# The second score matmul of the first layer's heads, run over all 128 rows

## The chip, the cores and the metric

The kernel runs on one core of a Trainium2 chip. The metric is the time of one execution in device microseconds (us). In the profile, PE is the matmul engine (TensorE) and PEld its weight loads, DVE is VectorE, ACT is ScalarE, POOL is GpSimd, and SP is the engine that issues most of the loads. The first operand of a matmul is held in the array (the weight load puts it there), the second streams past it; an array shape such as `64*128` in the profile says how many rows and columns of the array the instruction uses.

## The reference, cut to what matters

The program is an encoder of two layers over 256 tokens of 1024 values, all in float32. What the change touches is the attention of layer 0: sixteen heads of 64 values each, eight of mixer A (grouped queries, two key heads) and eight of mixer B (windowed, with a bias by distance).

```python
def gqa_attention(q, k, v):                     # mixer A
    ...
        logits = jnp.einsum('bqgrd,bkgd->bgrqk', qb, k).astype(jnp.float32) * scale
        p = jax.nn.softmax(logits, axis=-1).astype(v.dtype)
        return jnp.einsum('bgrqk,bkgd->bqgrd', p, v)

def dilated_attention(q, k, v, rel_bias):       # mixer B, for each of three branches
    ...
            logits = jnp.einsum('bqhd,bqkhd->bhqk', qb, kg).astype(jnp.float32) * scale
            logits = jnp.where(valid[None, None], logits + bias[None, :, None, :], NEG_INF)

# layer 0
proj = hn @ ab_w_in[j]
qa, ka, va, qb, kb, vb = jnp.split(proj, split_ab, axis=-1)
...
mix = jnp.concatenate([o_a, o_b], axis=-1) @ ab_w_out[j]
h = h + mix
h = h + jnp.square(jax.nn.relu(hn @ mlp_w1[layer])) @ mlp_w2[layer]
```

Layer 1 has a latent attention with sixteen heads and an MLP of the same form.

## The kernel before, in words

A value is kept as the sum of two parts, a high part in the short float type that the array takes at full pace (`fp32r`) and a low part, the rest. A product of two such sums is three matmuls into one bank (`mm3`, L263 to L265): high by high, high by low, low by high. The weights stream in as chunks of 1 MB on SP's queue, and ACT (L222) and DVE (L223) split each into its two parts, some quarters of a chunk ahead of use.

For the scores of a head (64 values) two matmuls do for three. `stack` (L708) puts the high part of a query head into its own half of the 128 rows (rows 0 to 63 for side s = 0, 64 to 127 for s = 1) and its low part into the other half. The high part of the keys stands in both halves (`kdA`, `kdB`). So the first score matmul (L847), over all 128 rows, gives (high + low of the query) by the high part of the key. The second (L848) uses only the 64 rows of the head's own half, `q[s][own, ...]`, and streams the low part of the keys in the same rows (`klA`, `klB`). Both are done for two blocks of 128 queries, so a head has four of them, in turn, into one bank `s`; 256 keys are 256 columns.

The low parts are written by one DVE operation over all 128 rows for mixer A (L775) and one for each pair of heads' half of mixer B (L820), each right behind an ACT copy of the high part over all 128 rows (L774, L819). In these tiles the rows of side 0 belong to even heads and those of side 1 to odd ones.

The heads run as a pipeline (`attention`, L340). In the turn of head h, PE transposes its normalised probabilities (L391), then scores head h + 2 (there are two `s` banks), and every second turn adds the weighted values of a pair of heads (L380), which use the array as `128*64`. DVE takes maxima (L418; L864 with the bias for mixer B) and normalises (L364); ACT takes the exponentials (L423, L873) and copies the transposes (L394). Between these, PE is given parts of a "filler" by head: the projections of mixer B's second half and its values, then the first half of the output projection (matmuls of 512 columns).

The order on each engine is laid out by a planner before the program runs: it goes by the order of the program text, raised or lowered by `high_priority` around some calls, and by its own costs of the instructions; the loops at the start are under `manual_schedule` and keep the written order. Engines run their queues in order.

The lines that the change touches: the tiles of layer 0 (L629, L633, L635, L641), the rotating buffer `work` (L195), `mixer_a_keys` (L771 to L778), the end of `qk_b` (L815 to L823), `scores_two` (L841) and its two callers (L853, L876). POOL fills the rotary tables `tab` from the loaded gains `gaq` and the constants `kc` (L725 to L730).

Of the kernel before, what the change touches and what calls it, by code (L numbers as in the profile page):

```python
# [20 lines left out]
P = 128  # L21
# [24 lines left out]
def shape_constants():  # L46
    """Rotary tables, the relative-position buckets and the branch counts: of the shapes alone."""
    f = np.float32
# [44 lines left out]
def weight_chunks():  # L93
    """The order in which the weights stream in: (name, columns used)."""
    order = [("qA", 0), ("qA", 1), ("kvA", 0)]
    order += [("qkB", i) for i in range(4)] + [("vB", 0), ("vB", 1)]
    order += [("outA", i) for i in range(4)]
    for l in range(2):
        if l == 1:
            order += [("down", 0), ("down", 1), ("uq", 0), ("uq", 1), ("ukv", 0)]  # L100
            order += [("outC", i) for i in range(4)]
        for u in range(17):
            if u < 16:
                order.append((f"w1_{l}", u))
            if u > 0:
                order.append((f"w2_{l}", u - 1))
    return order
# [11 lines left out]
def pack_weights(ab_w_in, ab_w_out, c_w_down, c_w_uq, c_w_ukv, c_w_out, mlp_w1, mlp_w2):  # L119
    """All weights in the order of their use, each chunk as 128 partition rows."""  # L120
    win, wout = ab_w_in[0], ab_w_out[0]
# [45 lines left out]
def encoder(ctx: ExitStack, tc: tile.TileContext, x, xt, wall, gcol, grow, const, onehot, relb, out):  # L167
# [26 lines left out]
    def work():  # L194
        return sp.tile([P, 512], F32, name="work", tag="work", bufs=6)  # L195

    def halves(z):
        return z.rearrange("p (m t) -> p m t", m=2)

# [1 line left out]
    raws, parts, done = {}, {}, set()  # L201
# [10 lines left out]
    def split_piece():  # L212
        """The next quarter of a chunk as two parts; of a chunk of the MLPs, the next half."""
        i, q = divmod(at["piece"], 4)
        n = 2 if i >= 5 else 1
        at["piece"] += n
        if q % 2 == 0:
            parts[i, q // 2] = [wp.tile([P, CW // 2], F32R, name=z, tag=z, bufs=W_BUFS) for z in ("whi", "wlo")]
        hi, lo = parts[i, q // 2]
        raw = raws[i][:, 512 * q:512 * (q + n)]  # L220
        s = slice(512 * (q % 2), 512 * (q % 2 + n))
        nc.scalar.copy(hi[:, s], raw)  # L222
        nc.vector.tensor_tensor(lo[:, s], raw, hi[:, s].bitcast(F32), op=OP.subtract)  # L223
        if q + n == 4:
            load(i + RAW_BUFS)
# [10 lines left out]
    def quarter(n=2):  # L236
        """A quarter of a chunk has been used."""
        at["quarter"] += 1
        pump(n)

    def take(name, j, n, whole=True):
        """A chunk of n row blocks: its operands by row block and columns."""
        i = at["take"]
        assert ORDER[i] == (name, j), (ORDER[i], name, j)
        at["take"] += 1
        while whole and at["piece"] < 4 * i + 4:
            split_piece()

        def operand(k, c=slice(None)):
            half, kk = divmod(k, n // 2)  # L250
            return tuple(z.rearrange("p (k c) -> p k c", k=n // 2)[:, kk, c] for z in parts[i, half])

        return i, operand
# [6 lines left out]
    def mm3(out, a, b, first, last):  # L260
        """out += a.T @ b, of operands that are each a sum of two parts."""
        (ah, al), (bh, bl) = a, b
        nc.tensor.matmul(out, ah, bh, start=first, stop=False)  # L263
        nc.tensor.matmul(out, ah, bl, start=False, stop=False)  # L264
        return nc.tensor.matmul(out, al, bh, start=False, stop=last)  # L265
# [6 lines left out]

# [1 line left out]
    g = cp.tile([P, N_G], F32, name="g")  # L274
# [32 lines left out]
    def rsqrt(u, n, dst):  # L307
        """u ** -0.5, with one Newton step behind the power."""
        y, z = (small(16)[:, :n] for _ in range(2))
# [11 lines left out]
    def mean_square(name):  # L321
        """mean(h * h) + eps, a column for each token block."""
        part, u = small(4), cp.tile([P, NT], F32, name=f"u{name}")
# [8 lines left out]
    def row_scales(bank, which, columns):  # L332
        """Values by token, spread over all partitions with the tokens along the row."""
        for t in range(NT):
# [3 lines left out]

# [1 line left out]
    def attention(heads, fill, dst):  # L340
# [34 lines left out]
        def values(j):  # L375
            """The weighted values of a pair of heads, side by side in the array."""
            ob = o_bank()
# [34 lines left out]
    def scaled_softmax(scale, nscale):  # L412
        """exp(scale * (s - max)) and its sums, the scale by query."""
        nb = {}
# [21 lines left out]
    def turn(c, t, gbase):  # L436
        """Half a token block of the residual stream, transposed, gained and split."""
        with tc.high_priority():
# [12 lines left out]
    class Later:  # L451
        """The turn of the last group, given out while the next one is computed."""
        todo = None
# [170 lines left out]

# [1 line left out]
    with tc.tile_pool(name="l0", bufs=1) as lp:  # L626
        qA = [lp.tile([P, 4, S], F32R, name=f"qA{s}") for s in range(2)]
        kdA = lp.tile([P, 2, S], F32R, name="kdA")
        klA = lp.tile([P, S], F32R, name="klA")  # L629
        vA = lp.tile([P, NT, P], F32, name="vA")  # L630
        qB = [lp.tile([P, 4, S], F32R, name=f"qB{s}") for s in range(2)]
        kdB = lp.tile([P, HB, S], F32R, name="kdB")
        klB = lp.tile([P, 4, S], F32R, name="klB")  # L633
        vB = lp.tile([P, NT, 512], F32, name="vB")
        tab = lp.tile([P, 4, NT, 64], F32, name="tab")  # L635
        rs_b = lp.tile([P, S], F32, name="rs_b")
# [3 lines left out]
        rq0 = lp.tile([P, NT], F32, name="rq0")  # L640
        gaq = lp.tile([P, P], F32, name="gaq")  # L641
        rb = lp.tile([NUM_BUCKETS + 1, HB], F32, name="rb")
# [5 lines left out]
        nc.vector.memset(rb, 1.0)  # L648
        nc.gpsimd.dma_start(rb[:NUM_BUCKETS, :], relb)

        # q, then k and v, of mixer A
        acc = [mm_bank() for _ in range(NT)]
# [37 lines left out]
        def load_bias(j):  # L690
            """rel_bias by distance, with the branch counts; query rows run backwards."""
            bias[j] = lp.tile([P, 2, 3 * P], F32, name="bias", tag="bias", bufs=2)
            nc.sync.dma_start(bias[j], bass.AP(tensor=line_d.tensor, offset=line_d.offset + 4 * S * j,
                                               ap=[[1, P], [2 * S, 2], [1, 3 * P]]))
# [13 lines left out]
        def stack(dst, src, col):  # L708
            """Rows of two heads, each as its high part beside its low part in the other rows."""
            for s in range(2):  # L710
# [49 lines left out]
        def mixer_a_keys(rk):  # L760
# [10 lines left out]
            for s in range(2):  # L771
                own, other = cols(s, 64), cols(1 - s, 64)
                if s == 0:
                    nc.scalar.copy(kdA[:, s], pk[:, :S])  # L774
                    nc.vector.tensor_tensor(klA, pk[:, :S], kdA[:, s].bitcast(F32), op=OP.subtract)  # L775
                else:
                    nc.scalar.copy(kdA[own, s], pk[own, :S])
                nc.scalar.copy(kdA[other, s], pk[own, :S])  # L778
            yield

        def qk_b(half, bank):
# [33 lines left out]
            for s in range(2):  # L815
                own, other = cols(s, 64), cols(1 - s, 64)
                hs = slice(4 * half + s, 4 * half + s + 3, 2)
                if s == 0:
                    nc.scalar.copy(kdB[:, hs], halves(kf))  # L819
                    nc.vector.tensor_tensor(klB[:, two], halves(kf), kdB[:, hs].bitcast(F32), op=OP.subtract)  # L820
                else:
                    nc.scalar.copy(kdB[own, hs], halves(kf[own]))
                nc.scalar.copy(kdB[other, hs], halves(kf[own]))  # L823
# [17 lines left out]
        def scores_two(q, kd, kl, s, j, order):  # L841
            own = cols(s, 64)

            def f(sb):
                for i in range(NT):
                    o = sb[:, cols(i, S)]
                    nc.tensor.matmul(o, q[s][:, j, cols(order[i])], kd, start=True, stop=False)  # L847
                    nc.tensor.matmul(o, q[s][own, j, cols(order[i])], kl, start=False, stop=True)  # L848
            return f

        def head_a(h):
            j, s = divmod(h, 2)
            return {"scores": scores_two(qA, kdA[:, s], klA[cols(s, 64)], s, j, (0, 1)),  # L853
                    "v": lambda c: vA[:, c, cols(s, 64)],
                    **scaled_softmax(fq[:, 2 * j + s], nfq[:, 2 * j + s])}

        def head_b(h):
# [13 lines left out]
            def ex(n, sb, p, l):  # L871
                for i in range(NT):
                    nc.scalar.activation(p[:, i], p[:, i], AF.Exp, bias=nb[0][:, i:i + 1],  # L873
                                         accum_out=l[:, i:i + 1])

            return {"scores": scores_two(qB, kdB[:, h], klB[cols(s, 64), j], s, j, (1, 0)), "max": mx, "exp": ex,  # L876
                    "v": lambda c: vB[:, c, cols(h, 64)], "flip": True}
# [44 lines left out]

# [1 line left out]
    with tc.tile_pool(name="l1", bufs=1) as lp:  # L924
# [194 lines left out]
```

## Time and profile before

| | before |
|---|---|
| time, median of 3 runs | 593.35 us (592.43 to 595.54) |
| profiled execution: span from its first to its last instruction | 591.9 us |
| profiled execution: its own time | not recorded; the span is 1.45 us under the median |
| PE busy | 578.0 us, 98% of the span |
| DVE, ACT, POOL busy | 364.7 (62%), 324.1 (55%), 35.0 us (6%) |
| mean granted TensorE clock | 0.994 of full speed |
| instructions | 8924 |

The profile is of one execution. Busy time of an engine is the time in which at least one of its instructions runs. Matmuls overlap: one may be listed with 0.28 us and the next start 0.12 us behind its start, so the pace of PE is read from the distances between starts, not from the durations. The heads of layer 0 lie between 53 and 120 us of the span, their scores between 53.1 and 104.1 us.

### The profile page before, as it was taken

How to read it: one execution, taken by the hardware profiler on the slowest of the kernel's cores; microseconds unless marked ns; L12 is line 12 of the kernel's file. 1: busy time of each engine (PE TensorE's matmuls, PEld its weight loads, DVE VectorE, ACT ScalarE, POOL GpSimd, SP SyncE). 2: the span in 40 equal slices, each digit the busy share in tenths (PEclk: the TensorE clock that was granted, in tenths of full speed). 3: DMA queues.
4: the chain of work that ended last, by engine and by line, in shares of the span. 5: the costliest groups of instructions: out<-in, count | busy, mean ns of one | idle time of the engine just before them, and what ended most of it. 6: DMA issues, size and time to landing. Idle time of an engine off the chain costs nothing.

```text
span 591.9 us, 8924 instructions
## 1 busy us (share of the span) xinstructions
PE 578.0 (98%) x3553; PEld 493.9 (83%) x3553; DVE 364.7 (62%) x583; ACT 324.1 (55%) x550; POOL 35.0 (6%) x70
## 2 busy tenths in 40 slices
PE   7989999999999999999999999999999999999994
PEld 3889665689998998898889987779899889989984
DVE  4888776586545546555468888757555645555425
ACT  5768875564444444435447498836444444544414
POOL 1480000000000000000002200000000000000003
PEclk9989999999999999999999999999999999999998
DMA  8955133135454555545544323146454554554201
GB/s 277 406 200 214 71 137 131 73 142 187 170 205 163 201 174 186 210 157 200 195 161 163 123 73 142 35 145 204 159 206 158 198 206 155 209 181 174 73 1 71
DMA packets 16602, 96.69 MB, mean 163 GB/s; under 512 B 1922, under 2 KB 3970, under 8 KB 5808
## 3 DMA queue, kind: packets, MB, share of 16 engines
q1 hardware_dynamic: 15984, 94.92, 43.9%
q0 software_dynamic: 288, 0.68, 0.5%
q8 instruction: 28, 0.46, 0.3%
q10 hardware_dynamic: 288, 0.52, 0.2%
q14 instruction: 14, 0.11, 0.1%
HBM read 95.05 MB, written 1.06 MB: 162 GB/s over the span
## 4 chain that ended last, share of the span: by engine, by line
PE 88%; ACT 3%; DMA 3%; DVE 2%; POOL 2%; issue 1%; SPq 1%; POOLq 0%; DVEq 0%; ACTq 0%
PE mm L263 15%; PE mm L264 15%; PE mm L265 14%; PE s L263 10%; PE s L264 10%; PE s L265 10%; PE o L380 3%; DMA raw<-in_wall 3%; PE o L391 3%; PE s L1075 2%; PE s L848 2%; PE s L847 1%; PE o L441 1%; DVE wlo L223 1%; ACT whi L222 1%
## 5 line engine op out<-in xcount | busy, mean ns | idle before, releaser
L223 DVE TENSOR_TENSOR wlo<-raw,whi 128x1024 fp32r<-128x1024 f32 (+1 forms) x182 | 208.9, 1165 | 150.3 <-ACT whi L222 150.1
L222 ACT CAST whi<-raw 128x1024 fp32r<-128x1024 f32 (+1 forms) x182 | 178.4, 1002 | 155.2 <-issue 66.3
L263 PE MATMUL s<-hT,whi 128*128 128x256 f32 x512 | 145.6, 284 | 0.0
L264 PE MATMUL s<-hT,whi 128*128 128x256 f32 x512 | 145.4, 284 | 0.0
L265 PE MATMUL s<-hT,wlo 128*128 128x256 f32 x512 | 145.2, 284 | 0.0
L264 PE MATMUL mm<-wlo,h2h 128*128 128x512 f32 x252 | 100.5, 399 | 0.0
L263 PE MATMUL mm<-whi,h2h 128*128 128x512 f32 x252 | 99.7, 396 | 0.0
L263 PEld LDWEIGHTS s<-hT,whi 128*128 128x128 f32 x512 | 98.4, 192 | 1.5
L264 PEld LDWEIGHTS s<-hT,whi 128*128 128x128 f32 x512 | 98.4, 192 | 1.3
L265 PEld LDWEIGHTS s<-hT,wlo 128*128 128x128 f32 x512 | 98.4, 192 | 0.1
L265 PE MATMUL mm<-whi,h2l 128*128 128x512 f32 x252 | 98.3, 393 | 0.0
L265 PEld LDWEIGHTS mm<-whi,h2l 128*128 128x128 f32 x252 | 47.3, 188 | 11.5 <-DVE h2l L514 0.4
L263 PEld LDWEIGHTS mm<-whi,h2h 128*128 128x128 f32 x252 | 47.4, 188 | 11.2 <-ACT h2h L513 0.7
L264 PEld LDWEIGHTS mm<-wlo,h2h 128*128 128x128 f32 x252 | 47.3, 188 | 9.5
L513 ACT CAST h2h<-work 128x512 fp32r<-128x512 f32 x32 | 19.9, 621 | 42.0 <-DVE work L510 42.0
L514 DVE TENSOR_TENSOR h2l<-work,h2h 128x512 fp32r<-128x512 f32 x32 | 22.2, 692 | 20.6 <-ACT h2h L513 20.6
L263 PE MATMUL mm<-whi,OT 128*128 128x512 f32 x64 | 26.9, 421 | 0.0
L510 DVE TENSOR_TENSOR work<-work 128x512 f32<-128x512 f32 x32 | 21.9, 685 | 7.7 <-ACT work L509 7.7
L264 PE MATMUL mm<-wlo,OT 128*128 128x512 f32 x64 | 25.8, 406 | 0.0
L265 PE MATMUL mm<-whi,OT 128*128 128x512 f32 x64 | 25.4, 401 | 0.0
L263 PE MATMUL mm<-whi,hT 128*128 128x512 f32 (+1 forms) x64 | 23.0, 360 | 2.3 <-ACT hT L663 2.2
L394 ACT COPY pts<-o 128x512 f32<-128x512 f32 x32 | 18.7, 589 | 10.9 <-PE o L391 10.8
(229 smaller groups left out, 770.6 us busy)
## 6 DMA issues: line engine op xcount, KB each, us to landing
raw<-in_wall SPq DMA_DIRECT2D x84, 1024.0 KB, 4.8
bias<-line_d SPq DMA_DIRECT2D x4, 384.0 KB, 3.5
raw<-in_wall SPq DMA_DIRECT2D x4, 256.0 KB, 5.5
raw<-in_wall SPq DMA_DIRECT2D x2, 512.0 KB, 7.7
xh<-in_x SPq DMA_DIRECT2D x1, 1024.0 KB, 10.7
xT<-in_xt SPq DMA_DIRECT2D x1, 512.0 KB, 6.9
kc<-in_const SPq DMA_DIRECT2D x1, 512.0 KB, 9.8
grw<-in_grow POOLq DMA_DIRECT2D x1, 512.0 KB, 4.8
```

What stands on the lines that cost most here:

```text
L222: nc.scalar.copy(hi[:, s], raw)
L223: nc.vector.tensor_tensor(lo[:, s], raw, hi[:, s].bitcast(F32), op=OP.subtract)
L263: nc.tensor.matmul(out, ah, bh, start=first, stop=False)
L264: nc.tensor.matmul(out, ah, bl, start=False, stop=False)
L265: return nc.tensor.matmul(out, al, bh, start=False, stop=last)
L380: nc.tensor.matmul(ob[64 * s:64 * s + 64, :S], heads[2 * j + s]["v"](c), pts[2 * j + s][:, cols(c, S)], start=c == 0, stop=c == NT - 1)
L391: turned = nc.tensor.transpose(pt[:, c * S + q * P:c * S + q * P + P], prob[h][:, i, cols(c)], flip if flipped else ident)
L394: nc.scalar.copy(pts[h], pt)
L510: nc.vector.tensor_tensor(r, r, r, op=OP.mult)
L513: nc.scalar.copy(hi, halves(r))
L514: nc.vector.tensor_tensor(lo, halves(r), hi.bitcast(F32), op=OP.subtract)
L848: nc.tensor.matmul(o, q[s][own, j, cols(order[i])], kl, start=False, stop=True)
```

## The change

The low parts of the keys get a tile row set for each side or head: `klA` has two entries of 256 columns instead of one, `klB` eight instead of four. In each, only the head's own half of the rows is written by DVE, and the other half is set to zero once, by POOL, at the start. The second score matmul then takes all 128 rows of the queries and of the low parts. The high parts are copied by halves of the rows for both sides, where side 0 used one copy over all rows before. The tables `tab` and `gaq` move into a tile `early` that shares its place with the second output tile `OT1`, and `work` has five buffers instead of six. Comment lines and docstrings are left out of the diff.

```diff
     def work():
-        return sp.tile([P, 512], F32, name="work", tag="work", bufs=6)
+        return sp.tile([P, 512], F32, name="work", tag="work", bufs=5)
...
         kdA = lp.tile([P, 2, S], F32R, name="kdA")
-        klA = lp.tile([P, S], F32R, name="klA")
+        klA = lp.tile([P, 2, S], F32R, name="klA")
...
-        klB = lp.tile([P, 4, S], F32R, name="klB")
+        klB = lp.tile([P, HB, S], F32R, name="klB")
         vB = lp.tile([P, NT, 512], F32, name="vB")
-        tab = lp.tile([P, 4, NT, 64], F32, name="tab")
+        early = ap.tile([P, 5 * P], F32, name="early", tag="OT1")
+        tab = early[:, :4 * P].rearrange("p (a t e) -> p a t e", a=4, t=NT)
+        gaq = early[:, 4 * P:]
...
-        gaq = lp.tile([P, P], F32, name="gaq")
...
         nc.gpsimd.dma_start(rb[:NUM_BUCKETS, :], relb)
+        for s in range(2):
+            other = slice(64 - 64 * s, 128 - 64 * s)
+            nc.gpsimd.memset(klA[other, s].bitcast(F32), 0.0)
+            nc.gpsimd.memset(klB[other, s::2].bitcast(F32), 0.0)
...
             for s in range(2):
                 own, other = cols(s, 64), cols(1 - s, 64)
-                if s == 0:
-                    nc.scalar.copy(kdA[:, s], pk[:, :S])
-                    nc.vector.tensor_tensor(klA, pk[:, :S], kdA[:, s].bitcast(F32), op=OP.subtract)
-                else:
-                    nc.scalar.copy(kdA[own, s], pk[own, :S])
+                nc.scalar.copy(kdA[own, s], pk[own, :S])
+                nc.vector.tensor_tensor(klA[own, s], pk[own, :S], kdA[own, s].bitcast(F32), op=OP.subtract)
                 nc.scalar.copy(kdA[other, s], pk[own, :S])
...
-                if s == 0:
-                    nc.scalar.copy(kdB[:, hs], halves(kf))
-                    nc.vector.tensor_tensor(klB[:, two], halves(kf), kdB[:, hs].bitcast(F32), op=OP.subtract)
-                else:
-                    nc.scalar.copy(kdB[own, hs], halves(kf[own]))
+                nc.scalar.copy(kdB[own, hs], halves(kf[own]))
+                nc.vector.tensor_tensor(klB[own, hs], halves(kf[own]), kdB[own, hs].bitcast(F32), op=OP.subtract)
                 nc.scalar.copy(kdB[other, hs], halves(kf[own]))
...
         def scores_two(q, kd, kl, s, j, order):
-            own = cols(s, 64)
-
             def f(sb):
                 for i in range(NT):
                     o = sb[:, cols(i, S)]
                     nc.tensor.matmul(o, q[s][:, j, cols(order[i])], kd, start=True, stop=False)
-                    nc.tensor.matmul(o, q[s][own, j, cols(order[i])], kl, start=False, stop=True)
+                    nc.tensor.matmul(o, q[s][:, j, cols(order[i])], kl, start=False, stop=True)
             return f
...
-            return {"scores": scores_two(qA, kdA[:, s], klA[cols(s, 64)], s, j, (0, 1)),
+            return {"scores": scores_two(qA, kdA[:, s], klA[:, s], s, j, (0, 1)),
...
-            return {"scores": scores_two(qB, kdB[:, h], klB[cols(s, 64), j], s, j, (1, 0)), "max": mx, "exp": ex,
+            return {"scores": scores_two(qB, kdB[:, h], klB[:, h], s, j, (1, 0)), "max": mx, "exp": ex,
```

## Rows read from the trace of the kernel before

**Rows 1.** The page: busy time by engine, and the chain that ended last.
```profile
PE 578.0 (98%) x3553; PEld 493.9 (83%) x3553; DVE 364.7 (62%) x583; ACT 324.1 (55%) x550; POOL 35.0 (6%) x70
...
PE 88%; ACT 3%; DMA 3%; DVE 2%; POOL 2%; issue 1%; SPq 1%; POOLq 0%; DVEq 0%; ACTq 0%
```

**Rows 2.** Stretches: length, each engine's busy time (instructions), clock, DMA share, GB/s.
```profile
59.66:87.81 28.15, 28.15 (x137) 18.76 (x135) 21.86 (x66) 22.27 (x54) 0.00 (x0) 1.00 0.28 95
53.10:104.10 51.00, 50.92 (x243) 33.50 (x242) 36.21 (x106) 37.41 (x91) 0.00 (x0) 1.00 0.38 139
...
87.81:96.24 8.43, 8.43 (x41) 5.30 (x40) 5.04 (x19) 6.35 (x18) 0.00 (x0) 1.00 0.39 152
96.24:102.85 6.61, 6.61 (x30) 3.47 (x28) 3.58 (x11) 2.83 (x7) 0.00 (x0) 1.00 0.41 159
```

**Rows 3.** PE's timeline: start, duration, line, operands, array shape, moving operand.
```profile
52.59 0.28 PE L265 MATMUL mm<-hT,wlo 128*128 128x256 f32 x1
52.71 0.28 PE L263 MATMUL mm<-hT,whi 128*128 128x256 f32 x1
...
59.66 0.28 PE L847 MATMUL s<-kdA,qA 128*128 128x256 f32 x1
59.88 0.38 PE L848 MATMUL s<-klA,qA 64*128 64x256 f32 x1
60.19 0.39 PE L847 MATMUL s<-kdA,qA 128*128 128x256 f32 x1
60.50 0.38 PE L848 MATMUL s<-klA,qA 64*128 64x256 f32 x1
60.81 0.50 PE L265 MATMUL mm<-whi,hT 128*128 128x512 f32 x1
61.15 0.40 PE L263 MATMUL mm<-whi,hT 128*128 128x512 f32 x1
61.38 0.39 PE L264 MATMUL mm<-wlo,hT 128*128 128x512 f32 x1
```

**Rows 4.** The second score matmul (L848): count, ns min/median/max, first and last start.
```profile
L848 PE MATMUL s<-klA,qA x16: 378/380/382, 53.5 to 77.6; 64*128 64x256 f32 x16
...
L848 PE MATMUL s<-klB,qB x16: 379/380/384, 79.9 to 103.8; 64*128 64x256 f32 x16
```

**Rows 5.** PE's timeline in head 14, weighted values and a low-part matmul.
```profile
99.19 0.65 PE L380 MATMUL o<-pts,vB 128*64 128x256 f32 x2
99.77 0.38 PE L848 MATMUL s<-klB,qB 64*128 64x256 f32 x1
```

**Rows 6.** Groups of 53.1 to 104.1 us, weight loads: busy us, mean ns | idle.
```profile
L264 PEld LDWEIGHTS mm<-hT,whi 128*128 128x128 f32 x6 | 1.1, 191 | 0.0
```

**Rows 7.** Timelines of PE and DVE: head 7's last score matmul and its normalisation.
```profile
77.64 0.38 PE L848 MATMUL s<-klA,qA 64*128 64x256 f32 x1
...
83.00 0.62 DVE L364 TENSOR_SCALAR prob<-prob,sm 128x256 f32<-128x256 f32 x2
```

**Rows 8.** Waits of 53 to 106 us: who <- for whom: us in total, times, longest.
```profile
ACT pts L394 <- PE o L391: 6.6, 10, 1.4
DVE sm L418 <- PE s L848: 4.6, 3, 1.8
```

**Rows 9.** The subtractions that write the low parts: count, ns min/median/max, starts.
```profile
L775 DVE TENSOR_TENSOR klA<-o,kdA x1: 425/425/425, 51.8 to 51.8; 128x256 fp32r<-128x256 f32 x1
...
L820 DVE TENSOR_TENSOR klB<-work,kdB x2: 684/688/691, 45.8 to 62.7; 128x512 fp32r<-128x512 f32 x2
```

**Rows 10.** POOL's timeline: a memset, and the rotary tables behind the idle time.
```profile
0.77 0.20 POOL L303 MEMSET ones<- 128x128 f32 x1
...
18.02 2.14 POOL L728 TENSOR_TENSOR tab<-kc,gaq 128x64 f32<-128x64 f32 x1 [14.87 <-DMA kc<-in_const]
...
20.55 0.31 POOL L728 TENSOR_TENSOR tab<-kc,gaq 128x64 f32<-128x64 f32 x1
```

**Rows 11.** Groups of 53.1 to 104.1 us: the splits' low parts on DVE.
```profile
L223 DVE TENSOR_TENSOR wlo<-raw,whi 128x1024 fp32r<-128x1024 f32 x11 | 13.3, 1219 | 0.0
```

## The prediction

> **What bounds the kernel now.** I began with the page: its first part gives each engine's share of the span, its fourth the chain of work that ended last. TensorE (PE) is busy for 578.0 of 591.9 us, and the chain is 88% PE [rows 1]. So a microsecond of PE work that disappears is worth up to a microsecond of the whole, wherever PE has no gaps. The table of busy time by stretch then shows the stage that the change touches: the sixteen heads of the first layer run from 53.1 to 104.1 us, and PE is busy for 50.92 of these 51.00 us; ACT and DVE are well under that, but not far (37.41 and 36.21) [rows 2].
>
> "Busy" is not "at full pace", so I read PE's timeline in that stretch by the distance from one start to the next. In an ordinary run of 256-column matmuls over 128 rows, starts are 0.12 us apart (52.59 to 52.71), and a 512-column one takes 0.23 (61.15 to 61.38) [rows 3]. Around the scores the pace is another: in head 2 the starts go 59.66, 59.88, 60.19, 60.50, 60.81, 61.15, so that four 256-column matmuls and the 512-column one behind them take 1.49 us instead of 4 x 0.12 + 0.23 = 0.71 [rows 3]. The slow steps are those at which the array changes between `128*128` and `64*128`, in either direction. The excess, 0.78 us over four changes, is 0.195 us a change.
>
> **The change part by part.**
>
> *The second score matmul over 128 rows.* There are 16 + 16 of these, all `64*128` today [rows 4], so 64 changes of shape at most. Going through the PE timeline head by head, 59 of them have a `128*128` neighbour on the other side and go away. Five have the weighted values there, which run as `128*64`: four around the two low-part matmuls of head 14 (99.77 stands right behind 99.19 [rows 5]) and one behind head 9, of the same kind; these stay changes of some kind, and I count nothing for them. 59 x 0.195 = 11.5 us of PE time. The bounds for the new matmul: a step of 0.12 us, as in the plain run, or 0.31 as today (59.88 to 60.19) [rows 3], which makes the gain 11.5 or 0. I take 0.12, because type, columns and rows are then the same as in the plain run. Twice as many rows is not twice as much work: the steps of that run are 0.12 with 128 rows in use.
>
> A weight load is one possible reason for the 0.31 that would not go away. The trace shows loads of 191 ns in the plain runs too, at steps of 0.12 [rows 3, 6]; they lie beside the matmul ahead.
>
> The Trainium skill ("TensorE: Matmul & The Clock Gate", Part 3, The mechanism) says that weight loads overlap running matmuls only when their row groups differ. By that rule a low-part matmul over all rows would show its load, and there would be nothing to gain; the trace does not agree, since rows of 128 everywhere go at 0.12.
>
> *How much of the 11.5 us is kept.* PE is the last to end only as long as ACT and DVE keep up, so I split the stage. Heads 0 and 1: 8 changes, 1.6 us; heads 2 to 10 (59.66 to 87.81): 35 changes, 6.8 us; heads 11 to 15: 16 changes, 3.1 us. In the middle part PE would need 28.15 - 6.8 = 21.3 us, while ACT needs 22.27 and DVE 21.86 [rows 2] plus 0.69 for one more subtraction (below), 22.55. So at most 28.15 - 22.55 = 5.6 us are kept there. The lower end comes from the handing round between engines: head 7's scores end at 78.02 (77.64 + 0.38) and its probabilities are normalised at 83.62, 5.6 us later [rows 7]; PE turns them two heads behind the scores. If that lag stayed, a head could not take less than 2.8 us, against 28.15 / 9 = 3.13 now: 9 x 0.33 = 3.0 us kept. I take 5.0, near the upper end, because much of ACT's and DVE's idle time is spent waiting for PE itself (6.6 us for the transposes, 4.6 for the last score matmul) [rows 8]; the lag shrinks when PE does. Behind 87.81, ACT has 6.35 of 8.43 us and then 2.83 of 6.61, DVE 5.04 and 3.58 [rows 2]; 3.1 us fit. Sum: 1.6 + 5.0 + 3.1 = 9.7 us.
>
> *More subtractions.* The low parts of the keys are now written once per half of the rows: three DVE operations become six, 0.43 us (A) and 0.69 (B) each [rows 9]; the fewer rows don't make one cheaper as I take it, since partitions run side by side. So 0.43 + 2 x 0.69 = 1.8 us more on DVE between 45 and 63 us. Cover: PE has projection matmuls to run meanwhile. I count 0 beyond the 0.69 already in the bound above; uncovered it costs 1.8. The ACT copies keep their number. A small gain lies here as well (the copy of the other half need no longer wait until DVE has read all rows of the first), which I leave at 0.
>
> *The zero rows.* Four memsets on POOL, two of 256 and two of 1024 columns. None like these is in the trace; a memset of 128 columns took 0.20 us, so in proportion 0.4 and 1.6 each, 4 us in all; if it were all fixed cost, 0.8; at the rate of a POOL tensor operation, 0.31 us for 64 columns, 12.4 us [rows 10]. I take 4, the same instruction. POOL stands idle for 14.87 us before 18.02, waiting for the table of constants [rows 10], and the program puts the memsets behind the three loads that POOL issues before that, so they delay none of these. The idle time hides all three figures; without this cover the rotary tables behind it, and all of POOL's norm factors, would come that much later.
>
> *Tables in the place of the second output tile, and 5 work tiles instead of 6.* The tables are last read before the heads begin, and that output tile is first written behind the values of heads 0 and 1; no wait. A work tile lives for a few operations; I see no place where more than four are in use. Both 0, and a microsecond either way because the planner lays out all queues anew.
>
> **Sum.** 591.9 - 9.7 = 582.2 us for the span. The profiled execution's own time is not recorded; its span is 1.45 us under the median of the three runs, 593.35, and I let that stand: 583.7 us.
>
> **The rivals.**
>
> *ACT and DVE become the bound and the lag stays.* Kept: 1.6 + 3.0 + 3.1 = 7.7, and less if it holds in the other heads too (15 heads x 0.33 = 5): 585.6 to 588.4. For it: the 22.55 against 21.3 above. Against: rows 8.
>
> *The slow step stays.* If a full-height weight load or the writing of the same bank is what takes 0.31, the 64 steps stay: 593.4, or 595 with DVE's 1.8 uncovered. Against it: the plain run does both, at 0.12.
>
> *Slower: a split of weights gets ahead of the normalisation.* The planner orders DVE's queue; each split of a weight block is 1.22 us [rows 11]. Were one more queued in front of the normalisation in each head, the lag would be 5.6 + 1.22 = 6.8 us, a head 3.4 us, and 15 heads 15 x (3.4 - 3.13) = 4 us longer: 597. It decides from a lag of 2 x 3.13 = 6.3 on; today there are 0.7 us to that. Against: these splits are as many as before, and must come somewhere.
>
> *All of it, and more.* With full use of the 11.5 us and a start of the heads a little earlier: 580 to 582.
>
> **How the numbers follow.** The forecast (582 to 585.5) gets 0.60, the lag 0.21, all and more 0.09, the slow step 0.05, slower 0.05. Half a percent, 2.97 us, is about what a measurement of this kernel tells from no change. Faster than 590.4: 0.60 + 0.21 + 0.09 = 0.90; within: 0.05, with some of the slower case 0.06; slower: 0.04. The range takes the forecast, the lag and most of the lower case: 580.8 to 588.8.
>
> **What would show it.** Right: the second score matmul listed as `128*128`, starts 0.12 us apart within a head's four, the four and their follower near 0.7 us; the stage from the first score to the last at 41 to 42 us instead of 51; ACT and DVE near nine tenths busy between heads 2 and 10, and PE with some small waits for normalised probabilities or copies. The lag would show as PE waits of 3 us and more ahead of the transposes. Wrong: steps that remain at 0.31; waits for the memsets; a shift of the time behind 125 us, which I hold to be unchanged.

## The result, and the profile after

The changed kernel takes 585.94 us (median; 585.39 to 586.45) against 593.19 us for the kernel before on the same chip: ratio 0.9869, 95% interval 0.9847 to 0.9891. The forecast was 583.7 us, in a range of 580.8 to 588.8. The direction and the range held; the gain is 7.25 us by the medians where 9.7 were forecast.

The page of the kernel after, busy time and chain (as in [rows 1]):

```profile
span 584.5 us, 8940 instructions
...
PE 570.0 (98%) x3553; PEld 491.5 (84%) x3553; DVE 366.0 (63%) x586; ACT 323.1 (55%) x550; POOL 36.7 (6%) x74
...
PE 87%; DVE 4%; ACT 2%; POOL 2%; DMA 1%; issue 1%; SPq 1%; POOLq 0%; DVEq 0%; ACTq 0%
```

PE lost 8.0 us of busy time, the span 7.4. It is still PE that ends last. Head 2 again, PE's timeline of the kernel after (as in [rows 3]: start, duration, line, operands, array shape):

```profile
59.05 0.39 PE L265 MATMUL mm<-whi,hT 128*128 128x512 f32 x1
59.27 0.30 PE L844 MATMUL s<-kdA,qA 128*128 128x256 f32 x1
59.41 0.28 PE L845 MATMUL s<-klA,qA 128*128 128x256 f32 x1
59.53 0.28 PE L844 MATMUL s<-kdA,qA 128*128 128x256 f32 x1
59.64 0.28 PE L845 MATMUL s<-klA,qA 128*128 128x256 f32 x1
59.76 0.40 PE L263 MATMUL mm<-whi,hT 128*128 128x512 f32 x1
60.00 0.40 PE L264 MATMUL mm<-wlo,hT 128*128 128x512 f32 x1
```

The four scores and their follower take 60.00 - 59.27 = 0.73 us, against 1.49 before; the working forecast 0.71. The steps between the scores are 0.11 to 0.14 us: a score matmul over 128 rows goes at the pace of the plain run, and its weight load adds nothing that shows. Counted over the whole run, neighbouring matmuls with different array shapes fell from 107 to 56, in the heads of layer 0 from 87 to 36.

But 36 is not the 28 that would be left of 87 less 59. Head 7, PE's timeline of the kernel after:

```profile
75.87 0.28 PE L844 MATMUL s<-kdA,qA 128*128 128x256 f32 x1
...
76.19 0.65 PE L380 MATMUL o<-pts,vA 128*64 128x256 f32 x2
76.77 0.55 PE L391 MATMUL o<-kc,prob 128*128 128x128 f32 x3
77.07 0.36 PE L845 MATMUL s<-klA,qA 128*128 128x256 f32 x1
77.36 0.65 PE L380 MATMUL o<-pts,vA 128*64 128x256 f32 x2
77.94 0.38 PE L844 MATMUL s<-kdA,qA 128*128 128x256 f32 x1
78.25 0.65 PE L380 MATMUL o<-pts,vA 128*64 128x256 f32 x2
78.83 0.39 PE L845 MATMUL s<-klA,qA 128*128 128x256 f32 x1
79.14 0.65 PE L380 MATMUL o<-pts,vA 128*64 128x256 f32 x2
```

The planner has threaded the scores of this head between the pieces of the weighted values (`128*64`). Each piece costs two changes of shape of its own, and more: from 78.25 to 79.14 one piece and one score matmul take 0.89 us, where three 256-column steps of the plain run are 0.36, so 0.26 us a change. Before, the values of layer 0 lay in 14 blocks, now in 18. PE's own waits in the heads of the kernel after are these two (who <- for whom: us in total, times, longest):

```profile
PE o L380 <- DVE OT L383: 0.8, 1, 0.8
...
PE o L391 <- DVE prob L364: 0.2, 1, 0.2
```

The stage from the first score to the last, and heads 2 to 10 of it, in the columns of [rows 2]:

```profile
54.88:98.90 44.02, 43.84 (x237) 31.11 (x236) 36.23 (x108) 37.71 (x93) 0.00 (x0) 1.00 0.43 159
59.27:87.47 28.20, 28.02 (x145) 19.54 (x145) 23.52 (x64) 23.43 (x56) 0.00 (x0) 1.00 0.38 136
```

The stage is 44.0 us long instead of 51.0 [rows 2]; 41 to 42 were forecast. Heads 2 to 10 by themselves did not get shorter, 28.20 us against 28.15: the new order puts 51 filler matmuls of 512 columns between them where there were 43. That is one reason why ACT and DVE are busy there for 83%, not the nine tenths that I expected. PE waits for 1.0 us in all. The side edits of the kernel after, by count, ns min/median/max and starts:

```profile
L653 POOL MEMSET klA<- x2: 305/306/307, 3.2 to 4.4; 64x256 f32 x2
L779 DVE TENSOR_TENSOR klA<-o,kdA x2: 409/418/428, 53.9 to 55.5; 64x256 fp32r<-64x256 f32 x2
...
L821 DVE TENSOR_TENSOR klB<-work,kdB x4: 683/686/690, 46.2 to 63.0; 64x512 fp32r<-64x512 f32 x4
...
L654 POOL MEMSET klB<- x2: 948/949/950, 3.4 to 4.7; 64x1024 f32 x2
```

The zero rows took 2 x 0.31 + 2 x 0.95 = 2.5 us (4 forecast) and lie in POOL's idle time; 12.49 us of it are left. The subtractions over 64 rows take as long as those over 128 did [rows 9].

### The profile page after: what moved, and what is told of

The parts are those of the page before. It is cut to its first block, busy times and chain, and to the rows that moved or that the text cites. A ratio compares the mean times of both kernels' runs of the same rounds, so it can differ in the third digit from the quotient of the medians.

```text
span 584.5 us, 8940 instructions
## 1 busy us (share of the span) xinstructions
PE 570.0 (98%) x3553; PEld 491.5 (84%) x3553; DVE 366.0 (63%) x586; ACT 323.1 (55%) x550; POOL 36.7 (6%) x74
## 4 chain that ended last, share of the span: by engine, by line
PE 87%; DVE 4%; ACT 2%; POOL 2%; DMA 1%; issue 1%; SPq 1%; POOLq 0%; DVEq 0%; ACTq 0%
PE mm L263 15%; PE mm L264 15%; PE mm L265 15%; PE s L263 10%; PE s L264 10%; PE s L265 10%; PE o L380 4%; PE o L391 3%; PE s L1072 2%; DVE wlo L223 1%; DMA raw<-in_wall 1%; PE o L441 1%; POOL sm L315 1%; PE s L844 1%; PE s L845 1%
## 5 line engine op out<-in xcount | busy, mean ns | idle before, releaser
L509 ACT ACTIVATE work<-s 128x512 f32<-128x512 f32 (+1 forms) x32 | 18.0, 562 | 8.9 <-PE s L265 8.9
```

Of the source, the lines that this page charges most:

```text
L509: nc.scalar.activation(r[:, cols(i, w)], b[:, :w], AF.Relu)
```

## The experiments

Two theories stood against each other. Mine: each change of array shape costs PE a fixed time, so the time follows the number of changes, and what the forecast lacked is the planner's new order. The rival, which the forecast itself had taken in half: ACT and DVE bound the middle heads, so that only a part of PE's saving is kept. "Changes" below are counted over the whole run; ratios are to the kernel before, with 95% intervals. Each ratio is taken to executions of the kernel before on the same chip as the row's own; beside all rows but the changed kernel their median was 595.3 to 595.4 us, not 593.19, so the medians of the table alone give slightly other gains.

| kernel | changes | median, us | ratio (interval) |
|---|---|---|---|
| before | 107 | 593.19 | |
| changed kernel | 56 | 585.94 | 0.9869 (0.9847 to 0.9891) |
| rows_alone | 48 | 582.85 | 0.9803 (0.9776 to 0.9830) |
| sides_alone | 111 | 594.49 | 1.0002 (0.9986 to 1.0017) |
| both_own_rows | 92 | 589.86 | 0.9923 (0.9896 to 0.9951) |
| values_in_one | 34 | 602.72 | 1.0138 (1.0111 to 1.0166) |
| scores_first | 40 | 581.64 | 0.9793 (0.9768 to 0.9818) |
| copies_first | 52 | 583.89 | 0.9827 (0.9803 to 0.9851) |
| one_copy_a | 48 | 584.19 | 0.9831 (0.9804 to 0.9859) |
| dve_more | 58 | 586.72 | 0.9881 (0.9851 to 0.9911) |
| dve_in_heads | 54 | 585.75 | 0.9849 (0.9826 to 0.9872) |
| act_in_heads | 52 | 584.26 | 0.9820 (0.9797 to 0.9843) |
| mlp_one_short | 168 | 606.80 | 1.0212 (1.0173 to 1.0252) |
| mlp_two_short | 168 | 606.97 | 1.0208 (1.0176 to 1.0239) |

**The rows alone, in the old order.**

```diff
...
-                    nc.tensor.matmul(o, q[s][own, j, cols(order[i])], kl, start=False, stop=True)
+                    nc.tensor.matmul(o, q[s][:, j, cols(order[i])], kl, start=False, stop=True)
...
-            return {"scores": scores_two(qA, kdA[:, s], klA[cols(s, 64)], s, j, (0, 1)),
+            return {"scores": scores_two(qA, kdA[:, s], klA, s, j, (0, 1)),
...
-            return {"scores": scores_two(qB, kdB[:, h], klB[cols(s, 64), j], s, j, (1, 0)), "max": mx, "exp": ex,
+            return {"scores": scores_two(qB, kdB[:, h], klB[:, j], s, j, (1, 0)), "max": mx, "exp": ex,
```

> The kernel before with one edit: the second score matmul takes all 128 rows, over the low parts as they lie (nothing is set to zero, so the other head's low parts enter the scores). All engine queues keep the order of the kernel before. Theory: each change of array shape costs PE some 0.195 us, and nothing else of the stage limits. 87 changes become 28, 59 fewer: 593.2 - 11.5 = 581.7 us, PE waits in the stage under 1 us. Rival: ACT and DVE bound the heads, so no more than the changed kernel's gain is kept: 586 us, with PE waits of 3 us and more ahead of the transposes.

Measured: 0.9803, that is 11.7 us of 593.19, where the theory had 11.5. PE's wait list has nothing of the heads in it. Heads 2 to 10 of this kernel, in the columns of [rows 2], and PE's and DVE's timelines of head 7, its last score matmul and its normalisation (as in [rows 7]):

```profile
57.40:79.10 21.70, 21.70 (x137) 16.49 (x135) 20.71 (x62) 21.20 (x53) 0.00 (x0) 1.00 0.33 118
...
71.31 0.28 PE L846 MATMUL s<-klA,qA 128*128 128x256 f32 x1
...
75.80 0.62 DVE L364 TENSOR_SCALAR prob<-prob,sm 128x256 f32<-128x256 f32 x2
```

With the same 43 filler matmuls as before, heads 2 to 10 became 28.15 - 21.70 = 6.45 us shorter, where the prediction kept at most 5.6. ACT is busy for 21.20 of the 21.70 us and DVE for 20.71, and PE still has no gap. The lag of head 7 is 76.42 - 71.59 = 4.8 us instead of 5.6, with the same operations in DVE's queue between the two. So nearly full side engines did not take anything back here. The rival's 586 is outside the interval. Not all of the 11.7 us is the rows': between the same two places in the two profiles, the first `mm<-hT,whi` of 256 columns and the first `o<-kc,xh` behind the heads, the gain is (123.43 - 49.37) - (111.61 - 48.52) = 11.0 us, 0.186 a change; most of the rest is the clock of an earlier stretch (last section).

**All the rest, without the rows.**

```diff
-                    nc.tensor.matmul(o, q[s][:, j, cols(order[i])], kl, start=False, stop=True)
+                    nc.tensor.matmul(o, q[s][cols(s, 64), j, cols(order[i])], kl[cols(s, 64)], start=False, stop=True)
```

> The changed kernel with one edit back: the second score matmul uses the head's own 64 rows again. Split subtractions, zero rows, the moved tables, five work tiles and the new order of the queues all stay. Theory: the order has 18 blocks of weighted values instead of 14, and with 64-row matmuls 91 changes of shape against 87: 4 x 0.195 = 0.8 us slower than before and up to 1.5 us of new waits, 594 to 595.5 us. Rival: the side edits (1.8 us of DVE, the zero rows) cost by themselves: 596 us and more. Second rival: they cost nothing: 593.2.

Measured: 594.49 us, ratio 1.0002. The median is where the theory had it, but the interval, 0.9986 to 1.0017, includes no difference at all: the extra subtractions, the zero rows, the moved tables, five work tiles instead of six and four more changes of shape together cost at most 1.0 us and gain at most 0.8 in this order. The gain is the rows'.

**Both score matmuls over 64 rows.**

```diff
-                    nc.tensor.matmul(o, q[s][:, j, cols(order[i])], kd, start=True, stop=False)
+                    nc.tensor.matmul(o, q[s][own, j, cols(order[i])], kd[own], start=True, stop=False)
```

> The kernel before with the first score matmul also over the head's own 64 rows (the low part of the queries is left out of the scores). Theory: the change of shape costs, not the 64-row matmul; the changes fall from 87 to 72, 15 fewer, so 590 to 591 us, and within a head the four matmuls start 0.12 us apart. Rival: a 64-row matmul is slow in itself (0.31 us from start to start): 64 of them instead of 32, at least 32 x 0.1 to 0.19 = 3 to 6 us slower, 596 to 599 us.

Measured: 589.86 us, just under the 590 to 591 expected, and faster with twice as many 64-row matmuls. PE's timeline of this kernel in head 2:

```profile
57.98 0.39 PE L847 MATMUL s<-kdA,qA 64*128 64x256 f32 x1
58.20 0.28 PE L848 MATMUL s<-klA,qA 64*128 64x256 f32 x1
58.32 0.28 PE L847 MATMUL s<-kdA,qA 64*128 64x256 f32 x1
58.44 0.28 PE L848 MATMUL s<-klA,qA 64*128 64x256 f32 x1
58.65 0.50 PE L263 MATMUL mm<-whi,hT 128*128 128x512 f32 x1
58.98 0.40 PE L264 MATMUL mm<-wlo,hT 128*128 128x512 f32 x1
```

Between neighbours of one shape the step is 0.12; it is 0.21 to 0.33 only where the group is entered and left. The 64-row matmul is not slow; coming to it and from it is.

**The price of a change by itself.** Two kernels change the MLPs' first product, far from the heads; `few` is rows 0 to 63 where k is 2, else all rows:

```diff
-                        rows(hb[:, cols(m, S)], w, m, ks)
...
+                            nc.tensor.matmul(o, ah, bh, start=k == 0, stop=False)
+                            nc.tensor.matmul(o, ah[ALL], bl[ALL], start=False, stop=False)    # mlp_one_short
+                            nc.tensor.matmul(o, ah[few], bl[few], start=False, stop=False)    # mlp_two_short
+                            nc.tensor.matmul(o, al[few], bh[few], start=False, stop=k == 7)
```

> The changed kernel with one matmul in each of 56 accumulations of the MLPs' first product (14 blocks of columns x 2 halves x 2 layers) over rows 0 to 63 only (that part of one low-by-high product is left out). The order of all queues is that of the changed kernel. No head is touched; 112 changes of shape come in, in runs that go at 0.12 us a step. Theory, a change costs 0.165 to 0.195 us wherever it stands: 18.5 to 21.8 us slower than the changed kernel, 604.4 to 607.7. Rival, the cost belongs to the scores (their bank, their operands): 586.

> As the run with one short matmul, but with two neighbours over rows 0 to 63 in each of the 56 places: 112 short matmuls and again 112 changes of shape. Theory: the change costs, not the short matmul: within 1.5 us of the run with one. Rival, each short matmul costs by itself: twice the excess, 623 us and more.

Measured: 606.80 and 606.97 us. 606.80 - 585.94 = 20.9 us for 112 changes, 0.187 us each (by the spans of the two profiles 604.9 - 584.5 = 20.4, 0.182 each); the second short matmul in a row adds nothing that shows. PE's timeline with one, then with two:

```profile
201.55 0.28 PE L531 MATMUL s<-hT,whi 128*128 128x256 f32 x1
201.76 0.38 PE L532 MATMUL s<-hT,wlo 64*128 64x256 f32 x1
202.07 0.38 PE L530 MATMUL s<-hT,whi 128*128 128x256 f32 x1
202.29 0.28 PE L531 MATMUL s<-hT,whi 128*128 128x256 f32 x1
202.41 0.28 PE L532 MATMUL s<-hT,wlo 128*128 128x256 f32 x1
```

```profile
201.07 0.28 PE L530 MATMUL s<-hT,whi 128*128 128x256 f32 x1
201.28 0.38 PE L531 MATMUL s<-hT,whi 64*128 64x256 f32 x1
201.51 0.28 PE L532 MATMUL s<-hT,wlo 64*128 64x256 f32 x1
201.71 0.38 PE L530 MATMUL s<-hT,whi 128*128 128x256 f32 x1
201.94 0.28 PE L531 MATMUL s<-hT,whi 128*128 128x256 f32 x1
```

With one, the steps are 0.21, 0.31 and 0.22 where the plain run has 0.12 three times: 0.38 us for going and coming back. With two, they are 0.21, 0.23, 0.20 and 0.23 where the plain run has 0.12 four times: 0.39 us again. Where in the row the time falls differs; the sum over the two changes is the same. This is the price of the prediction's [rows 3], in another stage, another bank and other operands. The Trainium skill ("TensorEngine Tiling (Array Packing)", Key Properties) says that changing the tiling mode drains the engine and changing only the tile does not. The trace agrees on the first, with 0.19 us a change; no run here changes the tile alone.

**Fewer blocks of values, by force.** In `attention`, orders on PE's queue (for both layers, since they share the function):

```diff
+                if behind is not None:
+                    order.enter_context(tc.issue_after(behind.ins))       # transposes behind the last values
...
-            with tc.high_priority(20):
-                scores(h + 2)
+            with tc.high_priority(20), tc.issue_after(turned.ins):
+                scored = scores(h + 2)
...
-                values(h // 2 - 1)
+                with tc.issue_after((scored or turned).ins):
+                    behind = values(h // 2 - 1)
```

> The changed kernel with the order on PE constrained: the weighted values of a pair of heads stand behind the scores of the head two ahead, and the next transposes behind the values. 18 blocks of values become 8, 36 changes of shape become 16. Theory: 20 x 0.195 = 3.9 us less than the changed kernel, 582 us; new waits of PE may take up to 2 us of it. Rival: ACT and DVE bound the heads: 586 us or more, the saved time turning into PE waits.

Measured: 602.72 us, 16.8 slower than the changed kernel, with the fewest changes of all. My theory allowed for 2 us of new waits. The rival's "586 us or more", with PE waits, holds by its words, though it foresaw the saved time turning into waits and not a loss. The longest of PE's wait list of this kernel:

```profile
PE o L396 <- DVE prob L364: 14.5, 13, 4.1
```

With no freedom to put something else first, PE stands ahead of the transposes (L396 here) until DVE has normalised: 14.5 us, 6.8 of it in layer 0 and the rest in layer 1. That is the lag of the prediction's first rival, and it is real; it costs PE time in this order, which leaves it nothing to do meanwhile, and nearly none in the others here. The blocks were put together at a price above their worth.

**Fewer blocks, by the planner's own means.** One number for the first, two small edits for the second:

```diff
-            with tc.high_priority(20):
+            with tc.high_priority(60):        # scores_first; 10 in copies_first
                 scores(h + 2)
```

```diff
                 nc.scalar.copy(kdA[own, s], pk[own, :S])
-                nc.vector.tensor_tensor(klA[own, s], pk[own, :S], kdA[own, s].bitcast(F32), op=OP.subtract)
                 nc.scalar.copy(kdA[other, s], pk[own, :S])
+                nc.vector.tensor_tensor(klA[own, s], pk[own, :S], kdA[own, s].bitcast(F32), op=OP.subtract)
```

> The changed kernel with one number changed: the scores' raise in the planner's order is 60 instead of 20 (both attentions). The planner then leaves the weighted values of layer 0 in 9 blocks instead of 18: 18 changes of shape instead of 36. Theory: 18 x 0.195 = 3.5 us less than the changed kernel at 585.9: 582.4 us, and as much more as new PE waits take (known to be possible from the run with the values forced into one block). Rival, ACT and DVE bound the heads: 586 us or more.

> The changed kernel with the key copies of mixer A ahead of the subtraction and the scores' raise at 10 instead of 20: also 18 changes of shape, in another order of the queues (45 alternations with transposes, where the run above has 47). Theory: 582.4 us plus new PE waits; if both kernels with 18 changes come out alike, the count of changes settles it, if they differ by more than 1 us, the waits in their orders do. Rival: 586 us or more.

Measured: 581.64 and 583.89 us. The first is the fastest kernel here and leaves nothing of the computation out; it is 4.3 us under the changed one (forecast 3.5), at 0.9793 of the kernel before. Its changes of shape are 16 fewer over the whole run, 3.0 us, and PE's waits in the heads 0.8 us less. A block of values of it, whole, and the matmul behind it:

```profile
69.52 1.08 PE L380 MATMUL o<-pts,vA 128*64 128x256 f32 x8
70.53 0.50 PE L264 MATMUL mm<-wlo,hT 128*128 128x512 f32 x1
```

Whole, the eight take 70.53 - 69.52 = 1.01 us; in head 7 of the changed kernel (above) each piece of two takes 0.58 (76.19 to 76.77), so four pieces 2.3. The program puts the two heads of a pair side by side in the array: in the single records of the whole block the matmuls start in pairs 0.01 us apart, in a piece of two 0.27 us apart. So a cut block also loses what ran side by side. Summed over the blocks of layer 0, from a block's first start to the start behind it, the values take 8.7 us here, 11.1 in rows_alone and 12.6 in the changed kernel.

The two differ by 2.3 us with the same 18 changes in layer 0, and I had put such a difference down to waits. That left something out: the raise is shared with layer 1, and at 10 its values fall into pieces too. Over the whole run copies_first has 52 changes and scores_first 40, 12 x 0.187 = 2.2 us. PE's waits in the heads are 1.0 and 0.2 us; the two together would be 3.0, more than was measured, and no run tells them apart.

**One subtraction's source.**

```diff
+                if s == 0:
+                    nc.scalar.copy(kdA[:, s], pk[:, :S])
+                    for z in range(2):
+                        nc.vector.tensor_tensor(klA[cols(z, 64), z], pk[cols(z, 64), :S],
+                                                kdA[cols(z, 64), 0].bitcast(F32), op=OP.subtract)
+                else:
+                    nc.scalar.copy(kdA[own, s], pk[own, :S])
```

> The changed kernel with the high parts of mixer A's keys copied over all 128 rows for side 0, as before the change, and both subtractions from that copy; the raise stays at 20. 28 changes of shape, the count that the edit of the rows alone left in the old order. Theory: 8 x 0.195 = 1.6 us less than the changed kernel and about 1 us less of waits if the old order's lack of them comes back: 583.3 to 584.4 us. Rival: 586.

Measured: 584.19 us, within the forecast. 14 blocks are back, as before the change, with one copy over all rows, and both subtractions from it, as the only edit: the planner's layout hangs on how mixer A's keys are written. It lies 1.3 us above rows_alone with the same 48 changes; the wait of 0.8 us ahead of the values stayed, and may be most of that.

**Is there room on ACT and DVE?** A first try missed its point:

```diff
+                nc.vector.tensor_scalar(extra[0], extra[0], 1.0, None, op0=OP.mult)    # ahead of norm(h + 1)
```

> The changed kernel with one more DVE operation of 128 x 256 in each of the sixteen heads, 16 x 0.27 to 0.35 = 4.3 to 5.6 us of DVE work (and four work tiles for space, which leaves the order alone); 38 changes of shape. Theory, DVE is not the bound: 0 to 1.5 us slower than the changed kernel, 586 to 587.5. Rival, ACT and DVE bound the heads: most of the added work shows, 589 to 591 us.

Measured: 586.72 us. But the operations depend on nothing in the heads, and the planner put all sixteen at the start:

```profile
L400 DVE TENSOR_SCALAR ex<-ex x16: 284/294/973, 1.5 to 11.7; 128x256 f32<-128x256 f32 x16
```

So this run says nothing about the heads. Tied to each head's probabilities, on DVE and on ACT:

```diff
+                ex = extra.tile([P, S], F32, name="ex")
+                nc.vector.tensor_scalar(ex, prob[h + 1][:, 0], 1.0, None, op0=OP.mult)   # dve_in_heads
+                nc.scalar.copy(ex, prob[h + 1][:, 0])                                    # act_in_heads
```

> The changed kernel with one more DVE operation in each of heads 1 to 15, tied to the head (a copy of 128 x 256 of its normalised probabilities that nobody reads; four work tiles for space): 15 x 0.27 to 0.35 = 4.0 to 5.3 us more on DVE between the scores. The planner's order has 54 changes of shape over the run instead of 56. Theory, PE bounds the heads and DVE has room: 585.9 - 2 x 0.187 = 585.5, with up to 1.5 us of new waits, 585 to 587. Rival, DVE bounds them: most of it shows, 589 to 591.

> The same with the copy on ACT, 15 x 0.27 to 0.37 = 4.0 to 5.6 us more on ACT; 52 changes of shape instead of 56. Theory, PE bounds the heads and ACT has room: 585.9 - 4 x 0.187 = 585.2, with up to 1.5 us of new waits, 584.5 to 586.7. Rival, ACT bounds them: 589 to 591.

Measured: 585.75 and 584.26 us, against 585.5 and 585.2 expected (584.26 lies 0.2 us under its range) and 589 to 591 by the rival. The added operations, by count, ns and starts:

```profile
L402 DVE TENSOR_SCALAR ex<-prob x15: 284/288/292, 64.5 to 104.2; 128x256 f32<-128x256 f32 x15
```

```profile
L402 ACT COPY ex<-prob x15: 394/408/428, 65.5 to 102.8; 128x256 f32<-128x256 f32 x15
```

4.3 us more on DVE and 6.1 us more on ACT added nothing: the times lie within 1 us of what the changes of shape give. Neither engine bounds the heads of the changed kernel.

## Why the prediction was right, and where not

*The price and the mechanism* were right. The excess read from the steps, 0.195 us a change, is 0.18 to 0.19 by the MLP runs, and the matmul over 128 rows goes at 0.12. The 59 changes and 11.5 us were right for the old order: rows_alone gave 11.7, or 11.0 where the earlier stretch is left out.

*"How much of the 11.5 us is kept"* failed as a reason. It took 1.8 us off for ACT and DVE in heads 2 to 10, from their busy sums and from head 7's lag. rows_alone lost nothing there: heads 2 to 10 took 21.70 us, less than the 22.27 us of ACT that the prediction said had to fit (its 22.55 had one subtraction more, which rows_alone does not have). ACT's work in them was 21.20 us in 53 instructions, where it had been 22.27 in 54, DVE's 62 instructions where it had been 66 [rows 2]: work moved over the edges of the stretch, so a busy time read between two points of the old order is no floor for the new one. The lag did not stay either. Head 7's 5.6 us became 4.8, and it was no fixed measure before: head 9's scores ended at 83.26 and its probabilities were normalised at 92.12, 8.9 us later, far above the 6.3 from which a lag was to decide, and PE did not wait. What sets the lag of a head was not tried by itself.

*"A microsecond either way because the planner lays out all queues anew"* is the term that was mis-sized. Between rows_alone and the changed kernel lie 3.1 us by the medians and 4.4 by the spans (580.1 and 584.5). Of the 4.4, 8 more changes are 8 x 0.187 = 1.5 and PE's waits 1.0. Some 0.8 more is the clock (below). The values take 12.6 - 11.1 = 1.5 us longer in more pieces; less the way out of four more blocks, 4 x 0.187, some 0.7 us of that are not yet in the changes (an estimate). The last 0.4 us stays open.

So a loss of 1.8 us taken off for the wrong cause stood in for one of 4.2 us of other causes (11.5 - 7.25), and the forecast came out 2.2 us low. That it came so near is in part luck.

*The covers at nothing* (zero rows, subtractions, moved tables, work tiles) held: sides_alone, 1.0002. *The slow step stays* fell with the 0.12 steps, *slower* with the time itself. The Trainium skill ("TensorE: Matmul & The Clock Gate", Part 3, The mechanism) says that weight loads overlap running matmuls only when their row groups differ; the trace of the changed kernel does not agree, as the score matmuls over all rows start 0.11 to 0.14 us apart.

## What to carry to other kernels

Read PE's pace from the distances between starts, and look for short or narrow matmuls among full ones: here each change of array shape costs 0.19 us, as much as one and a half 256-column matmuls, so zero rows that keep the shape are cheaper than leaving rows out. Short ones next to each other in the queue pay for the change only on the way in and out. A small edit can also move a planner's whole order, here for 3.1 us of the 11.7 that the rows alone gave: count in the new order what the gain depends on before trusting the old one. Nor is an engine's busy time between two points of the old order a floor: 22.27 us of ACT were to fit, and the stretch went down to 21.70. Forcing the order cost 16.8 us where 20 changes, 3.7 us, were to be saved; one priority saved 18 of the 20 in the same heads.

## What the runs showed of the hardware that I had not expected

The time of one kernel depends on a stretch that the change does not touch. PE waits 1.9 us near 37 us of the span. That stretch in the kernel before and in rows_alone, in the columns of [rows 2], and PE's timeline behind the wait in the kernel before:

```profile
30.00:44.00 14.00, 12.12 (x91) 11.91 (x90) 11.60 (x18) 9.18 (x16) 12.20 (x27) 0.88 0.55 198
30.00:44.00 14.00, 12.11 (x101) 11.73 (x100) 11.78 (x19) 10.49 (x17) 12.14 (x27) 1.00 0.60 202
...
40.58 0.41 PE L265 MATMUL s<-hT,wlo 128*128 128x256 f32 x1
40.79 0.41 PE L263 MATMUL s<-hT,whi 128*128 128x256 f32 x1
...
42.13 0.28 PE L264 MATMUL s<-hT,whi 128*128 128x256 f32 x1
42.24 0.28 PE L265 MATMUL s<-hT,wlo 128*128 128x256 f32 x1
```

In the profiles of the kernels before and after the mean granted clock of 30 to 44 us is 0.88: behind that wait 256-column steps are 0.21 instead of 0.12 us, until 41.9, which is the lower of the two levels, 1.2 instead of 2.4 GHz. In the profile of rows_alone, with the same wait, it is 1.00; why was not tried. Of the changed kernel's four runs, those with a mean clock of 0.997 and 0.998 took 585.66 and 585.39 us, those with 0.991 and 0.992 586.23 and 586.45, so some 0.8 us go with it; the kernel before, on the chip of rows_alone, goes from 592.74 us at 0.997 to 596.80 at 0.990. A difference of a microsecond between two single runs here can be the clock alone.
